# Loading a transpose's row blocks with every fourth row in the same quarter of the partitions, and mending the order with a permutation

## The chip, the cores and the metric

The kernel runs on one core of a Trainium2 chip. The metric is the device time in microseconds (us), the median of several runs. The core has engines with queues of their own, named as in the profile: TensorE (PE, with PEld for its weight loads), VectorE (DVE), ScalarE (ACT), GpSimd (POOL) and SyncE (SP). Transfers between the chip's memory and the core's on-chip memory run on 16 DMA engines, whichever queue issues them.

## The reference

The input is one matrix of 8192 x 8192 float32 (32 KB for a row, 268 MB in all). The output is its transpose.

```python
def reference(x: np.ndarray) -> np.ndarray:
    return np.transpose(x)
```

## The kernel before

The input is taken in 128 chunks `(s, c)`. Chunk `c` of strip `s` is a block of P = 128 rows (64 blocks, `CH`) by `J` = 4096 columns (two strips), so 2 MB, 16 KB in each of the 128 partitions. `load(t)` (L101) brings chunk `t` into one of `NIN` = 3 buffers `ins`, row `p` of the block into partition `p`. The first three loads are issued by SyncE, all others by ScalarE (L103).

`transposes(k)` (L112) waits until the semaphore of buffer `k` stands at 18: 16 from the transfer, and one each from ScalarE and VectorE, which say that they have emptied what the chunk before left in PSUM. Then TensorE transposes 32 blocks of 128 x 128, each by a matmul with the identity `ident` (L117). The columns of a block are taken in steps of `B` = 4, so that one partition of the result holds four neighbouring columns of `x`, which are four neighbouring rows of the output. `ident` is made by GpSimd at the start, from a memset and one select (L85, L87). TensorE's part is a loop with a register, the other engines' queues are written out in full.

ScalarE (for the first half, `e` = 0) and VectorE (`e` = 1) copy the results from PSUM into one of `NREG` = 9 regions of `regs` (L241). A region gathers one group of 512 output rows over up to `W` = 8 chunks; the eight groups are staggered, so that in the middle of the run about one region is complete after each chunk. `store` (L154) then writes it out, 2 MB at a time for full regions, 16 KB for each partition, to four output rows in pieces of up to 4 KB. All stores are issued by ScalarE.

In ScalarE's queue a store of chunk `t` waits until TensorE has begun chunk `t+1` (in the middle of the run), and `load(t + 3)` follows right behind it (L264). The transfers that ScalarE issues are thus ordered store, load, store, load, one pair for a chunk. SyncE waits for the last stores at the end (L266).

Transfers are made in two ways. `dma_start` needs the same shape on both sides. `wide_dma` (L25) adds the transfer instruction itself and hands it both access patterns as they are, with a count of 1 put in where a side has two dimensions only (`physical`), so the sides may have different shapes. All stores but the first go that way.

Of the kernel before, what the change touches and what calls it, by code (L numbers as in the profile page):

```python
# [8 lines left out]
def physical(ap):  # L9


    t = ap.tensor
    dims = [list(d) for d in ap.ap]
    if len(dims) == 2:
        dims.insert(1, [dims[1][1], 1])
    return mybir.PhysicalAccessPattern(
        ap=dims,
        offset=ap.offset,
        dtype=ap.dtype,
        memref=t.name,  # L20
        memsetref=t.name + "_set",
    )


def wide_dma(nc, eng, queue, out, in_):  # L25


    return eng.add_instruction(
        mybir.InstDMACopy(
            mode="Copy",  # L30
            name=nc.get_next_instruction_name(),
            engine=eng.engine,
            ins=[physical(in_)],
            outs=[physical(out)],
            queue=queue,
        )
    )
# [3 lines left out]
def kernel(  # L41
# [13 lines left out]
    nc = tc.nc  # L55
    P = 128
# [8 lines left out]
    NIN = 3  # L65
    NREG = 9
    CH = N // P
    J = S * P

    with tc.tile_critical():  # L70
        nc.alloc_sbuf_tensor("pad", [P, 32], dt)
        ident = nc.alloc_sbuf_tensor("ident", [P, P], dt).ap()
        ins = [nc.alloc_sbuf_tensor(f"in{k}", [P, J], dt).ap() for k in range(NIN)]
        SIZE = B * W * P
# [4 lines left out]
        s_id = nc.alloc_semaphore("s_id")  # L79
        s_ld = [nc.alloc_semaphore(f"s_ld{k}") for k in range(NIN)]  # L80
# [3 lines left out]

        nc.gpsimd.memset(ident, 0.0).then_inc(s_id, 1)  # L85
        nc.gpsimd.wait_ge(s_id, 1)
        nc.gpsimd.affine_select(  # L87
            out=ident,
            in_=ident,
            compare_op=mybir.AluOpType.not_equal,  # L90
            fill=1.0,
            base=0,
            pattern=[[-1, P]],
            channel_multiplier=1,
        ).then_inc(s_id, 1)
        nc.vector.sem_inc(s_ld[0], 1)
        nc.scalar.sem_inc(s_ld[0], 1)

        chunks = [(s, c) for s in range(M // J) for c in range(CH)]

        def load(t):  # L101
            s, c = chunks[t]
            (nc.sync if t < NIN else nc.scalar).dma_start(  # L103
                out=ins[t % NIN], in_=x[c * P:(c + 1) * P, s * J:(s + 1) * J]
            ).then_inc(s_ld[t % NIN], 16)

# [16 lines left out]
        T = len(chunks)  # L125
        assert T % NIN == NIN - 1
        pe = [nc.tensor.engine]
        nc.tensor.wait_ge(s_id, 2)

        turn = nc.alloc_registers("turn", engines=pe)  # L130
        nc.regs_mov(turn, 0)
# [11 lines left out]
        for t in range(NIN):  # L143
            load(t)
# [9 lines left out]
        def store(q, e, t):  # L154
# [7 lines left out]
            for s, a, z in parts:  # L162
                rows = (z - a) * P
                j0 = s * J + q * B * P
                dst = out[j0:j0 + B * P, a * P:a * P + rows]
# [19 lines left out]
        for t, (s, c) in enumerate(chunks):  # L185
            closed = []
            for e in range(2):
                eng = (nc.scalar, nc.vector)[e]
# [4 lines left out]
                for q in range(e * NH, (e + 1) * NH):  # L193
# [14 lines left out]
                    base = r * SIZE + B * P * sum(z - a for _, a, z in parts[:k])  # L208
# [52 lines left out]
            if t + NIN < T:  # L261
                if not closed:
                    nc.scalar.wait_ge(s_pe, (t + 1) * NH)
                load(t + NIN)  # L264
# [32 lines left out]
```

## Time and profile before

| | |
|---|---|
| median of 3 runs | 1261.94 us (1261.61 to 1261.95) |
| profiled execution, first to last instruction (span) | 1260.4 us |
| profiled execution, around the span, as median less span | 1.5 us |
| read from and written to memory | 268.44 MB and 268.44 MB |
| transfers issued | 270 |

The profile is of one execution. Its times are in us from the span's start unless they are marked ns; a row of a group of instructions gives their busy time, the mean of one, and the idle time of the engine ahead of them with what ended it. Rows of stretches give each engine's busy time with the number of instructions in brackets, the clock that TensorE was granted (1.00 is full speed), the busy share of the DMA engines and their rate. Rows of transfers give their number, the KB of one, and the median time from issue to landing. Registers, branches, semaphores and the issuing of transfers are not counted as busy.

### The profile page before, as it was taken

To read this page: it belongs to the slowest core of one execution; us is meant where nothing else is said; L and a number is where in the kernel's file an instruction comes from. 1 tells how busy PE (TensorE), PEld (TensorE's weight loads), DVE (VectorE), ACT (ScalarE), POOL (GpSimd) and SP (SyncE) were. 2 spreads that over 40 slices of the span, in tenths; PEclk is the share of its full clock that TensorE was granted. 3 is DMA by queue.
4 is the path that set the end of the run, shared out by engine and by line. 5 is a ranking of instruction groups with operands and counts; after the bars stand their busy time and mean duration, and the time that the engine had idled before them with its cause. 6 is when DMAs were issued, how large, how long until landed. Compare 5 with 4: busy or idle time off the path is not lost. (4 is left out here: it accounts for less than half of the span.)

```text
span 1260.4 us, 9367 instructions
## 1 busy us (share of the span) xinstructions
PE 739.0 (59%) x4096; PEld 718.4 (57%) x4096; DVE 302.0 (24%) x250; ACT 253.5 (20%) x257; POOL 0.7 (0%) x6
## 2 busy tenths in 40 slices
PE   5656556565566655565556656566565655665561
PEld 5556556565556655565555656565565655665561
DVE  2322222222222222222222222222222222222220
ACT  3212211122111211122111211121111211121110
POOL 0000000000000000000000000000000000000000
PEclk9886876868777777778687786867777687777776
DMA  9999999999999999999999999999999999999998
GB/s 383 429 422 426 425 430 431 426 431 431 427 430 431 428 428 431 428 429 432 427 422 426 429 429 425 431 429 428 430 428 428 431 428 429 429 429 429 429 431 376
DMA packets 39271, 536.95 MB, mean 426 GB/s; under 512 B 4320, under 2 KB 4832, under 8 KB 6240
## 3 DMA queue, kind: packets, MB, share of 16 engines
q10 hardware_dynamic: 38832, 530.60, 99.0%
q1 hardware_dynamic: 432, 6.29, 1.2%
q14 instruction: 6, 0.05, 0.0%
q8 instruction: 1, 0.02, 0.0%
HBM read 268.44 MB, written 268.44 MB: 426 GB/s over the span
## 5 line engine op out<-in xcount | busy, mean ns | idle before, releaser
L117 PE MATMUL ps<-ident,in 128*128 128x128 f32 x4096 | 739.0, 362 | 493.5 <-PEq L113 493.5
L117 PEld LDWEIGHTS ps<-ident,in 128*128 128x128 f32 x4096 | 718.4, 220 | 513.9 <-issue 513.9
L241 DVE COPY regs<-ps 128x512 f32<-128x512 f32 (+3 forms) x250 | 302.0, 1246 | 932.1 <-PE ps L117 932.1
L241 ACT COPY regs<-ps 128x512 f32<-128x512 f32 (+3 forms) x256 | 252.2, 1016 | 978.8 <-PE ps L117 760.8
L241 ACT ACT_TABLE_LOAD x1 | 1.3, 1283 | 1.0 <-SPq L70 1.0
L87 POOL TENSOR_SCALAR_AFFINE_SELECT ident<-ident 128x128 f32<-128x128 f32 x1 | 0.3, 293 | 0.2 <-POOL ident L85 0.2
L85 POOL MEMSET ident<- 128x128 f32 x1 | 0.2, 204 | 0.5 <-SPq L70 0.5
L281 POOL MEMSET const-bfloat16-1.0<- 128x1 bf16 x1 | 0.1, 102 | 0.0
L281 POOL MEMSET const-uint8-127<- 128x1 uint8 x1 | 0.1, 102 | 0.0
L281 POOL MEMSET const-float32-0.0<- 128x1 f32 x1 | 0.1, 99 | 0.2 <-issue 0.2
L281 POOL MEMSET const-float32-1.0<- 128x1 f32 x1 | 0.1, 99 | 0.0
## 6 DMA issues: line engine op xcount, KB each, us to landing
in<-in_x_dram ACTq DMA_DIRECT2D x125, 2048.0 KB, 16.8
out_dram<-regs ACTq DMA_DIRECT2D x114, 2048.0 KB, 12.6
out_dram<-regs ACTq DMA_DIRECT2D x4, 1792.0 KB, 11.1
in<-in_x_dram SPq DMA_DIRECT2D x3, 2048.0 KB, 11.7
out_dram<-regs ACTq DMA_DIRECT2D x4, 1536.0 KB, 12.5
out_dram<-regs ACTq DMA_DIRECT2D x4, 1280.0 KB, 11.5
out_dram<-regs ACTq DMA_DIRECT2D x4, 1024.0 KB, 11.1
out_dram<-regs ACTq DMA_DIRECT2D x4, 768.0 KB, 12.3
```

The costliest lines, as they stand in the source:

```text
L85: nc.gpsimd.memset(ident, 0.0).then_inc(s_id, 1)
L87: nc.gpsimd.affine_select(out=ident, in_=ident, compare_op=mybir.AluOpType.not_equal, fill=1.0, base=0, pattern=[[-1, P]], channel_multipl ...
L117: tr = nc.tensor.transpose(pss[e][:, (g * B + b) * P:(g * B + b + 1) * P], ins[k][:, q * B * P + b:(q + 1) * B * P - B + b + 1:B], ident,)
L241: cp = nc.scalar.copy(out=o, in_=i) if e == 0 else nc.vector.tensor_copy(out=o, in_=i)
L281: nc = _bacc.Bacc("TRN2", target_bir_lowering=False, num_devices=1)
```

## The change

In the loads, row `4 l + h` of a block now goes to partition `32 h + l`, for `h` from 0 to 3 and `l` from 0 to 31: each quarter of the partitions holds every fourth row. The source of a load is therefore a pattern of three dimensions, `(l h) j -> h l j`, with counts 4, 32 and 4096, and the loads after the first are made with `wide_dma`. Load 0 is split into four transfers of 32 partitions by 4096 elements; the first of them counts on the buffer's semaphore, the other three on a new one, `s_l0`, on which VectorE waits before its first signal to TensorE.

TensorE undoes the new order as it transposes: `ident` is no longer the identity but the permutation with a one in row `32 h + l` and column `4 l + h`, made with four selects of 32 partitions instead of one of 128. The transposes, copies and stores stay as they are.

```diff
+    H = 4
+    L = P // H
...
-        nc.gpsimd.affine_select(
-            out=ident,
-            in_=ident,
-            compare_op=mybir.AluOpType.not_equal,
-            fill=1.0,
-            base=0,
-            pattern=[[-1, P]],
-            channel_multiplier=1,
-        ).then_inc(s_id, 1)
+        for h in range(H):
+            nc.gpsimd.affine_select(
+                out=ident[h * L:(h + 1) * L, :],
+                in_=ident[h * L:(h + 1) * L, :],
+                compare_op=mybir.AluOpType.not_equal,
+                fill=1.0,
+                base=h,
+                pattern=[[-1, P]],
+                channel_multiplier=H,
+            ).then_inc(s_id, 1)
+        s_l0 = nc.alloc_semaphore("s_l0")
+        nc.vector.wait_ge(s_l0, 16 * (H - 1))
         nc.vector.sem_inc(s_ld[0], 1)
         nc.scalar.sem_inc(s_ld[0], 1)
...
         def load(t):
             s, c = chunks[t]
-            (nc.sync if t < NIN else nc.scalar).dma_start(
-                out=ins[t % NIN], in_=x[c * P:(c + 1) * P, s * J:(s + 1) * J]
-            ).then_inc(s_ld[t % NIN], 16)
+            src = x[c * P:(c + 1) * P, s * J:(s + 1) * J].rearrange("(l h) j -> h l j", h=H)
+            if t == 0:
+                for h in range(H):
+                    nc.sync.dma_start(out=ins[t][h * L:(h + 1) * L], in_=src[h]).then_inc(s_ld[0] if h == 0 else s_l0, 16)
+            else:
+                eng, queue = (nc.sync, "qSPDynamicHW") if t < NIN else (nc.scalar, "qActDynamicHW")
+                wide_dma(nc, eng, queue, ins[t % NIN], src).then_inc(s_ld[t % NIN], 16)
...
-        nc.tensor.wait_ge(s_id, 2)
+        nc.tensor.wait_ge(s_id, 1 + H)
```

## The prediction

> **What bounds the kernel now.** I read the page's busy shares and slices first, then the packets and queues, then stretches of the span, then the waits, and last the instructions in order of time.
>
> ```profile
> span 1260.4 us, 9367 instructions
> PE 739.0 (59%) x4096; PEld 718.4 (57%) x4096; DVE 302.0 (24%) x250; ACT 253.5 (20%) x257; POOL 0.7 (0%) x6
> DMA  9999999999999999999999999999999999999998
> GB/s 383 429 422 426 425 430 431 426 431 431 427 430 431 428 428 431 428 429 432 427 422 426 429 429 425 431 429 428 430 428 428 431 428 429 429 429 429 429 431 376
> DMA packets 39271, 536.95 MB, mean 426 GB/s; under 512 B 4320, under 2 KB 4832, under 8 KB 6240
> q10 hardware_dynamic: 38832, 530.60, 99.0%
> q1 hardware_dynamic: 432, 6.29, 1.2%
> HBM read 268.44 MB, written 268.44 MB: 426 GB/s over the span
> ```
>
> No computing engine is busy for more than 59% of the span, while the two transfer queues together keep the 16 DMA engines busy for 100%. The bytes are the least possible: 268.44 MB in and 268.44 MB out. So the time is bytes over rate, and the rate is flat:
>
> ```profile
> core 0: us, PE busy (x) PEld busy (x) DVE busy (x) ACT busy (x) POOL busy (x), PEclk, DMA share, GB/s
> 0.00:31.50 31.50, 17.80 (x128) 17.16 (x128) 8.57 (x14) 9.81 (x16) 0.70 (x6) 1.00 0.94 383
> 31.50:330.00 298.50, 178.50 (x1003) 173.52 (x1004) 73.57 (x52) 61.21 (x59) 0.00 (x0) 0.77 1.01 428
> ...
> 990.00:1229.00 239.00, 143.27 (x777) 139.43 (x778) 58.36 (x49) 46.89 (x45) 0.00 (x0) 0.75 1.01 429
> 1229.00:1260.40 31.40, 3.49 (x24) 3.30 (x23) 2.48 (x4) 2.34 (x4) 0.00 (x0) 0.61 0.90 377
> ```
>
> Only the first and the last 31 us are below a full share. Between them the share is 1.01 and the rate 428 to 429 GB/s, 26.8 GB/s for one engine. One engine moves 536.9/16 = 33.55 MB; at 428.2/16 = 26.76 GB/s that is 1253.7 us, and the other 6.7 us of the span are its two ends. The median of the runs, 1261.94 us, is 1.5 us over this span; I add that at the end.
>
> The waits agree: TensorE waits before each of the 128 chunks (the sequencer's wait on the loads), and SyncE does nothing but wait for stores.
>
> ```profile
> PE ps L117 <- PEq L113: 493.5, 128, 8.4
> SPq L266 <- DMA out_dram<-regs: 1256.8, 4, 1248.1
> ```
>
> **The change, part by part.** *How loads are cut into pieces.* Every transfer must be shared out over the 16 DMA engines. What before shows of that is a count:
>
> ```profile
> in<-in_x_dram ACTq DMA_DIRECT2D x125, 2048.0 KB, 16.8
> out_dram<-regs ACTq DMA_DIRECT2D x114, 2048.0 KB, 12.6
> out_dram<-regs ACTq DMA_DIRECT2D x4, 1792.0 KB, 11.1
> in<-in_x_dram SPq DMA_DIRECT2D x3, 2048.0 KB, 11.7
> ...
> out_dram<-regs ACTq DMA_DIRECT2D x4, 256.0 KB, 12.1
> ```
>
> There are 125 + 3 loads and 114 + 7 x 4 = 142 stores (seven smaller sizes, 1792 to 256 KB), 270 transfers, and 4320 packets under 512 B: exactly 16 for each transfer. I read these as one completion mark for each engine that took part, so each transfer of before ran in 16 pieces. In the code all 270 have a leading count of 128 or 512 on both sides, a multiple of 16. The simplest rule that fits is that a transfer is cut along the leading counts of its two sides, into a number of pieces, at most 16, that divides both.
>
> The change breaks the condition. Loads 1 to 127 now have the source `(l h) j -> h l j`: its leading count is H = 4, then 32 rows, then 4096 elements; the destination still leads with 128 partitions. Cut along leading counts, these loads make 4 pieces, one for each `h`: 32 rows of 16 KB on one engine. Sixteen pieces of eight partitions, which would start 32 rows x 32 KB = 1 MB apart, need the 4 and the 32 to be taken together. Load 0 is four transfers with a leading count of 32 on both sides, so it stays on 16 engines. The stores are untouched.
>
> [...]
>
> [...] A transfer in 16 pieces uses every engine, so before can't show which ones a smaller number takes; I take the same ones each time, as the simpler case, and keep the other as a rival. With k pieces on the same k engines, one of these engines carries 268.44/16 = 16.78 MB of stores and, for each of loads 1 to 127, 2.097/k MB, and 0.13 MB of load 0.
>
> For k = 4: 127 x 2.097/4 = 66.58 MB; with 16.78 and 0.13 it is 83.49 MB, 2.5 times as much as before. At 26.76 GB/s: 3119.9 us. With the ends, 6.7 us: a span of 3126.6 us. With 1.5 us around it: **3128 us**. For k = 16 it is before's 33.55 MB and 1260.4 us of span. In between there is no gentle case: k = 8 gives (16.78 + 33.43)/26.76 = 1876 us.
>
> Bounds on k = 4: the fastest slice, 432 GB/s or 27.0 GB/s for an engine, gives 3092 + 8 = 3100 us; no row shows one engine working with others idle, so I allow another 1% below. Above, the four engines must never run dry. What feeds them is ACT's queue:
>
> ```profile
> 610.74 6.12 PEld L117 LDWEIGHTS ps<-ident,in 128*128 128x128 f32 x32 [3.86 <-issue]
> 610.77 6.28 PE L117 MATMUL ps<-ident,in 128*128 128x128 f32 x32 [3.69 <-PEq L113]
> 612.75 0.55 ACTq L28 DMA_DIRECT2D out_dram<-regs  x1
> 613.34 0.61 ACTq L103 DMA_DIRECT2D in<-in_x_dram  x1
> 613.98 2.05 ACT L241 COPY regs<-ps 128x512 f32<-128x512 f32 x4 [7.72 <-issue]
> 617.08 2.48 DVE L241 COPY regs<-ps 128x512 f32<-128x512 f32 x4 [7.49 <-PE ps L117]
> ```
>
> When chunk t+1 has landed (610.7), the store of t and load t+3 are issued within 613.95 - 610.74 = 3.2 us. At that moment the store of t-1 and load t+2 are still queued: on a loaded engine 2.097/16/26.76 = 4.9 us and 2.097/4/26.76 = 19.6 us. A chunk is then 24.5 us, and TensorE (6.3), the copies and the issue (3.2) fit in it side by side. So these engines have over 20 us of work in hand, and I take no bubble. If they ran dry for the 3.2 us in every chunk, it would cost 127 x 3.2 = 406 us and end at 3530 us. What could do it is an issue that blocks: in the last stretch five store issues take 15.33 us in all, since the queues are full there.
>
> ```profile
> 1233.38 15.33 ACTq L28 DMA_DIRECT2D out_dram<-regs  x5
> ```
>
> [...]
>
> *The permutation, its wait and the split load 0.* These lie at the start:
>
> ```profile
> 0.94 1.32 SPq L103 DMA_DIRECT2D in<-in_x_dram  x3
> 1.38 0.29 POOL L87 TENSOR_SCALAR_AFFINE_SELECT ident<-ident 128x128 f32<-128x128 f32 x1 [0.23 <-POOL ident L85]
> 8.37 5.34 PEld L117 LDWEIGHTS ps<-ident,in 128*128 128x128 f32 x32 [8.37 <-issue]
> 13.94 0.36 ACTq L103 DMA_DIRECT2D in<-in_x_dram  x1
> ```
>
> Four selects in place of one are at most 4 x 0.29 us, 0.9 us more on POOL, done before 3 us; TensorE starts at 8.37 on load 0, so the price is nothing, and 0.9 us without that cover. SyncE issues six transfers instead of three, 3 x 0.44 = 1.3 us more, which puts loads 1 and 2 off, not the first piece. DVE's wait on `s_l0` has only DVE's sem_inc and its first copies behind it, and TensorE needs load 0 whole anyway. If load 0 lands 1 to 5 us later (its four pieces in turn, each a quarter of the partitions), the engines that decide still have loads 1 and 2 to carry, 39 us for k = 4: nothing. For k = 16 only two loads x 4.9 us are behind it and up to 2 us could show. The 4096 transposes keep their number, shape and order, and a permutation in place of the identity has the same operands.
>
> **The rivals.** *A: sixteen pieces after all, not slower.* The place is each load's split: if the inner 32 is taken with the 4, every engine gets eight rows, 33.55 MB as before, and the order in memory alone changes. It decides only at k = 16; at k = 8 the time is already 1876 us. For it speaks that 128 rows are there to be shared. Its gain is what ripple there is: the 38 inner slices average 428.4 GB/s, the usual best is 431, so 0.6% of 1197 us, 7 us, if loads caused all of it: 1255 us. If they caused none, 1262 us, with the first load's 0 to 2 us on top up to 1264. Against any large gain speaks that the engines are already full.
>
> *B: sixteen pieces, but reads 128 KB apart within an engine collide in memory.* All stores already write over that pitch at full rate, which speaks against it. If all slices fell to the slowest inner one, 422 instead of 428.2, it is 1.5%: 1281 us.
>
> *C: four pieces that go to other engines from load to load.* Then the stress spreads; with two loads in flight on eight engines the loaded ones would need about k = 8's 1876 us. Nothing in before rules it out; nothing shows it.
>
> **How the numbers follow.** A gets 0.10, B 0.02, C 0.03, and the four fixed engines 0.85: the counts in the code put a 4 where every transfer that was seen in 16 pieces had a multiple of 16, and cutting the leading count is the one rule that needs no regrouping. The time is that of four engines, 3128 us. The range is 3070 (the fastest slice's rate less 1%) to 3300 (under half of the dry-engine bound); I give it 0.95 if the four engines hold, so 0.81 in all. A measurement of this kernel can tell about 0.2%, 2.5 us, from no change. Slower: 0.85 + 0.02 + 0.03, and 0.01 from A; A leaves 0.06 for faster and 0.03 for the same.
>
> **What would show it.** Right: a mean rate of 537/3.127 = 172 GB/s and a DMA share about 0.4 (four engines full, twelve with 16.9 of 83.5 MB); packets under 512 B down from 4320 to 142 x 16 for stores, 4 x 16 for load 0 and 127 x 4: 2844; chunks of 24.5 us; TensorE's waits before a chunk near 18 us; a load about 46 us from issue to landing (two loads and two stores deep, 49 us, less the 2.6 from landing to issue). Wrong: 4320 + 48 tiny packets and a share of 1 (A or B); chunks well above 24.5 us with the share under 0.4 (dry engines); between 1500 and 2200 us (C). If the tiny packets are 2844 but one engine's rate differs from 26.76 GB/s, the cut was right and the rate was mis-sized.

## The result and the profile after

The changed kernel takes 3134.26 us (3133.94 to 3136.26) where the kernel before took 1261.78 us beside it: 2.484 times as long (95% interval 2.481 to 2.487). The prediction said 3128 us, in 3070 to 3300.

The page of the changed kernel, by the same rows as before: span and busy shares, the 40 slices of the DMA engines and their rate, packets, queues (q10 is ScalarE's, q1 SyncE's).

```profile
span 3132.4 us, 9376 instructions
PE 763.7 (24%) x4096; PEld 743.0 (24%) x4096; DVE 302.2 (10%) x250; ACT 252.8 (8%) x257; POOL 1.6 (0%) x9
DMA  3333334433443334433344333433344333443335
GB/s 105 151 166 167 168 168 183 171 168 168 173 183 168 168 167 177 180 168 168 168 186 170 168 167 168 186 168 168 168 178 178 168 168 167 181 176 168 168 171 249
DMA packets 37795, 536.95 MB, mean 171 GB/s; under 512 B 2844, under 2 KB 3356, under 8 KB 4764
q10 hardware_dynamic: 37332, 530.59, 39.8%
q1 hardware_dynamic: 456, 6.29, 0.7%
HBM read 268.44 MB, written 268.44 MB: 171 GB/s over the span
```

The bytes are the same, but the 16 engines are busy for 40% of the span in the mean instead of 100%. The small packets tell why: 2844 instead of 4320, which is 16 for each of the 142 stores and the four parts of load 0, and 4 for each of the other 127 loads. In a stretch from the middle, in order of time (start, duration, engine, what; idle time before in brackets):

```profile
1515.20 6.06 PE L126 MATMUL ps<-ident,in 128*128 128x128 f32 x32 [18.06 <-PEq L122]
1517.18 0.57 ACTq L28 DMA_DIRECT2D out_dram<-regs  x1
1517.79 0.58 ACTq L28 DMA_DIRECT2D in<-in_x_dram  x1
...
1539.50 5.89 PE L126 MATMUL ps<-ident,in 128*128 128x128 f32 x32 [18.24 <-PEq L122]
...
1563.79 5.71 PE L126 MATMUL ps<-ident,in 128*128 128x128 f32 x32 [18.41 <-PEq L122]
```

A chunk takes 24.3 us instead of 9.8. TensorE works for 6 us and waits 18 us for the next load. ScalarE issues here as promptly as before (0.57 and 0.58 us), so no issue blocks: the loaded engines set the pace. At the start the four parts of load 0 delay TensorE, and the next chunk comes late:

```profile
13.28 6.09 PE L126 MATMUL ps<-ident,in 128*128 128x128 f32 x32 [13.28 <-PEq L122]
46.69 6.39 PE L126 MATMUL ps<-ident,in 128*128 128x128 f32 x32 [27.32 <-PEq L122]
```

### The profile page after: what moved, and what is told of

The parts are those of the page before. It is cut to its first block, busy times and chain, and to the rows that moved or that the text cites. A ratio compares the mean times of both kernels' runs of the same rounds, so it can differ in the third digit from the quotient of the medians.

```text
span 3132.4 us, 9376 instructions
## 1 busy us (share of the span) xinstructions
PE 763.7 (24%) x4096; PEld 743.0 (24%) x4096; DVE 302.2 (10%) x250; ACT 252.8 (8%) x257; POOL 1.6 (0%) x9
## 2 busy tenths in 40 slices
DMA packets 37795, 536.95 MB, mean 171 GB/s; under 512 B 2844, under 2 KB 3356, under 8 KB 4764
## 3 DMA queue, kind: packets, MB, share of 16 engines
q10 hardware_dynamic: 37332, 530.59, 39.8%
## 5 line engine op out<-in xcount | busy, mean ns | idle before, releaser
L126 PE MATMUL ps<-ident,in 128*128 128x128 f32 x4096 | 763.7, 371 | 2341.5 <-PEq L122 2341.5
L126 PEld LDWEIGHTS ps<-ident,in 128*128 128x128 f32 x4096 | 743.0, 220 | 2361.9 <-issue 2361.9
```

What stands on the lines that cost most here:

```text
L126: tr = nc.tensor.transpose(pss[e][:, (g * B + b) * P:(g * B + b + 1) * P], ins[k][:, q * B * P + b:(q + 1) * B * P - B + b + 1:B], ident,)
```

## The experiments

The theory is that the leading counts of a transfer's two sides set the number of engines, and that loads with a leading 4 use the same four each time. The rivals: something else in the change costs the time (the form of the transfer, the permutation, the start), or the distance between the rows that one engine reads does.

**All of the change but the leading 4.**

```diff
-                wide_dma(nc, eng, queue, ins[t % NIN], src)...
+                wide_dma(nc, eng, queue, ins[t % NIN], x[c * P:(c + 1) * P, s * J:(s + 1) * J])...
```

> All of the change is kept (permutation, s_l0, load 0 in four transfers, wide_dma for loads 1 to 127), only the source of loads 1 to 127 is taken in its own row order again, so its leading count is 128 and not 4. (The rows within a block of 128 then stand in the permuted order in the output; times are not touched by that.) Theory, the cut follows the leading counts: 16 pieces again, 1262 us within 4 us, tiny packets 142 x 16 + 4 x 16 + 127 x 16 = 4368, DMA share about 1. Rival, the cost lies in wide_dma's form, the permutation or the start: it stays near 3134 us.

It took 1265.78 us, 1.0035 (1.0021 to 1.0049) of before, with the 4368 small packets forecast:

```profile
DMA packets 39319, 536.95 MB, mean 425 GB/s; under 512 B 4368, under 2 KB 4880, under 8 KB 6288
0.00:31.50 31.50, 14.38 (x96) 13.90 (x96) 6.29 (x11) 7.73 (x13) 1.56 (x9) 1.00 0.95 328
31.50:1229.00 1197.50, 721.08 (x3968) 701.07 (x3968) 293.35 (x236) 243.55 (x240) 0.00 (x0) 0.75 1.01 429
```

The second and third row are stretches of its span (busy times, granted clock, DMA share, GB/s). The middle is that of before; the 3.9 us that remain are the start, 328 GB/s in the first 31.5 us against 383. So the form of the transfer and the permutation cost nothing that can be seen, the start with its split load 0 about 4 us, and the leading 4 all the rest.

**Only the leading 4, rows and identity as before.** All loads go by `wide_dma` here and in the experiments with another H below, so a small `dma_start` into the unused tile `pad` stands ahead of them on SyncE's queue; the permutation is made by selects over all partitions, or is the identity (H = 1).

```diff
...
+            src = x[c * P:(c + 1) * P, s * J:(s + 1) * J].rearrange("(k l) j -> k l j", k=4)
...
```

> Rows in the order of the kernel before, with the identity; only the source pattern is written with leading counts 4 and 32 (32 neighbouring rows for each of 4 pieces). Theory, the leading count alone decides: 16.78 + 67.11 = 83.89 MB on an engine, 3135 us and with the ends 3143, within 15. Rival, the order of the rows in memory has a share in the changed kernel's 3134 us: lower than that by over 1%.

The one run took 3139.86 us, with 2928 small packets: 142 x 16 + 128 x 4, and 128 + 16 of the small transfer. The reordering of the rows has no part in the loss.

**Two pieces and eight pieces.** The second kernel has H = 8 in the same place.

```diff
-    H = 4
+    H = 2
...
```

> H = 2 in place of 4: every second row in the same half of the partitions; all loads by wide_dma, behind a small transfer into an unused tile; the permutation from selects over all partitions. Theory, cut along the leading count on the same engines each time: 2 pieces, 16.78 + 128 x 2.097/2 = 151.0 MB on an engine, at 26.76 GB/s 5642 us and with the ends 5650 us; tiny packets 142 x 16 + 128 x 2 + 16 = 2544; chunks 44.1 us. Rival, what costs is the distance between the rows that an engine reads (64 KB here, 128 KB with H = 4, 32 KB before): under 3134 us. Rival, pieces on engines that change from load to load: well under 5650 us.

> H = 8. Theory, cut along the leading count: 8 pieces, 16.78 + 33.55 = 50.33 MB on an engine, 1881 us and with the ends 1889 us; tiny packets 142 x 16 + 128 x 8 + 16 = 3312. Rival, the distance between the rows that an engine reads (256 KB here): over 3134 us.

In one run each, H = 2 took 5607.58 us, 0.75% under its forecast, and H = 8 1922.55 us, 1.8% over; small packets 2672 and 3440, the forecasts plus the 128 of the small transfer. If distance between rows were what costs, H = 2 would have been the fastest of the three, and it is the slowest. The bytes of the busiest engine order all of them. That H = 2 needs the full 5.6 ms also means that its pieces do not move over to idle engines from load to load.

At the start the number of engines is seen directly. From 4 to 22 us only the first loads move, on SyncE's queue. The rows give packets, MB and the share of 16 engines, for H = 2, for the leading 4 with the rows of before, and for H = 8; the last line is H = 8's rate by slices:

```profile
q1 hardware_dynamic: 60, 0.98, 12.7%
q1 hardware_dynamic: 70, 1.15, 24.9%
q1 hardware_dynamic: 137, 2.11, 50.5%
GB/s 121 160 263 273 290 289 281 286 297 281 281 292 291 281 283 300 280 281 294 290 280 281 297 283 281 284 300 281 281 294 289 280 286 297 281 281 294 289 303 305
```

These are 2, 4 and 8 engines of 16, although with 4 and 8 pieces all three first loads had been issued by 3.5 us. One engine moved 0.98 MB in 0.127 x 16 x 18 us, 26.8 GB/s, with two pieces, but by the same sum only 16.0 with four and 14.5 with eight. The slices of H = 8 show this slow start, and that it passes; it is why H = 8 came out over its forecast. Why it passes no run here shows.

**Sixteen pieces.**

```diff
-    H = 4
+    H = 16
...
```

> H = 16: the leading count is 16, so by the theory 16 pieces of 8 rows that lie 512 KB apart, 33.55 MB on every engine: 1262 us, tiny packets 142 x 16 + 128 x 16 + 16 = 4336. Rival, distance between rows: slower than H = 8. Second rival: with this cut an engine has 8 neighbouring partitions, and if engines then meet at the same part of the on-chip memory as load 0's four transfers seem to in the changed kernel (first transposes at 13.2 instead of 8.4 us), loads run at down to half rate: between 1262 and 1889 us.

The four runs took 1745, 1752, 1822 and 1852 us, inside the range of the second rival (1262 to 1889), though the cut is in 16 (4464 small packets, 4336 + 128). The page of the run of 1745 us:

```profile
span 1743.3 us, 9400 instructions
DMA  9999999999999999999999999999999999999998
DMA packets 39415, 536.97 MB, mean 308 GB/s; under 512 B 4464, under 2 KB 4976, under 8 KB 6384
q10 hardware_dynamic: 38832, 530.60, 98.3%
```

All engines are busy all the time, as before, yet move 308 GB/s. By the queue's row, 16 KB take 0.983 x 16 x 1743.3 us x 16 KB / 530.60 MB = 0.85 us of an engine, against 0.62 by the same row of before. So packets are held up while they count as busy. Two things may be at work: rows of one engine are 512 KB apart instead of 32 (theory M, memory), or, if the cut follows the leading 16, each engine has eight neighbouring partitions and engines meet there (theory P, on-chip memory). The next two kernels separate them. The first has the rows of before (H = 1).

```diff
...
+            src = x[c * P:(c + 1) * P, s * J:(s + 1) * J].rearrange("(k l) j -> k l j", k=16)
...
```

> Rows in the order of the kernel before, with the identity; only the source pattern is written with leading counts 16 and 8 (eight neighbouring rows for each of 16 pieces) and all loads go by wide_dma, behind a small transfer into an unused tile. It asks why H = 16 took 1745 to 1852 us with full engines and packets of 16 KB at a mean of 0.86 us instead of 0.61. Theory P, engines meet in on-chip memory, because a cut in 16 along a leading 16 gives each engine eight neighbouring partitions: the same here, 1740 to 1860 us. Theory M, it is memory, rows of one engine 512 KB apart with H = 16: here they are 32 KB apart as before, so 1262 us.

```diff
-    H = 4
+    H = 32
...
```

> H = 32: leading counts 32 and 4; every 32nd row, 1 MB apart, goes to the same four neighbouring partitions. Packets 142 x 16 + 128 x 16 + 16 under 512 B plus some 128 for the small transfer, so 16 pieces. [...] Theory P with a plain cut of 32 in 16 (eight neighbours again): 1740 to 1860 us. Theory M: rows 1 MB apart, no faster than H = 16, over 1740 us.

With rows next to each other but a leading 16, so by theory P eight neighbouring partitions for each engine: 1770.02 us. With rows 1 MB apart and a leading 32, for which 1262 us within 5 was forecast if the engines do not meet: 1271.44 us. Pages of the first and the second:

```profile
DMA packets 39415, 536.97 MB, mean 305 GB/s; under 512 B 4464, under 2 KB 4976, under 8 KB 6384
```

```profile
GB/s 312 411 426 429 426 430 430 429 428 428 429 431 429 431 429 430 428 429 430 429 424 427 429 431 429 430 428 430 430 430 427 430 430 430 430 430 428 430 428 365
DMA packets 39416, 536.98 MB, mean 424 GB/s; under 512 B 4464, under 2 KB 4976, under 8 KB 6384
```

Theory M fails on both. Theory P fits both only if with a leading 32 or 128 the engines get their partitions otherwise than with 16. That was the author's assumption: no trace shows which partitions an engine serves, or where engines meet. Measured are the times, 1745 to 1852 us with a leading 16 against 1262 with 128 and 1271 with 32.

The start shows the loads by themselves. From 4 to 13 us nothing moves but the first loads: in the kernel before, with the leading 16 and the rows of before, with H = 32, and in the first experiment, where load 0 is in four parts:

```profile
q1 hardware_dynamic: 267, 3.85, 99.9%
q1 hardware_dynamic: 136, 2.00, 103.2%
q1 hardware_dynamic: 256, 3.93, 102.0%
q1 hardware_dynamic: 185, 1.98, 99.1%
```

All engines are full in all four, and in the second and the fourth they move half the bytes. No store takes part, so the pieces of the loads hold each other up; it is not the neighbours in one engine as such, since with H = 2 each engine had 64 of them by the same cut and ran at 26.8 GB/s. The four parts of load 0 are of this kind, and that is where the 4 us of the first experiment went.

**The change's order of rows, on 16 engines, by four transfers for each load.**

```diff
+            for h in range(H):
+                (nc.sync if t < NIN else nc.scalar).dma_start(
+                    out=ins[t % NIN][h * L:(h + 1) * L], in_=src[h]
+                ).then_inc(s_ld[t % NIN], 16)
...
+            nc.tensor.sem_inc(s_ld[k], -16 * H - 2).wait_op(s_ld[k], 16 * H + 2, "sem-ge")
```

> The changed kernel's order of rows and its permutation, but each load made as load 0 is: four transfers of 32 partitions, each with a leading count of 32 on both sides, so 16 pieces; a buffer's semaphore counts to 66. Tiny packets 142 x 16 + 512 x 16 = 10464. If the number of pieces were all: 1262 to 1275 us. [...]

By theory P, with loads at down to half rate, 1700 to 1890 us were forecast, since load 0 made this way landed 4.9 us late. Two runs took 1714.49 and 1810.51 us. The engines are full and slow again; the page is of the longer run:

```profile
span 1808.7 us, 9757 instructions
q10 hardware_dynamic: 44832, 530.62, 98.7%
DMA packets 45418, 537.00 MB, mean 297 GB/s; under 512 B 10464, under 2 KB 10976, under 8 KB 12384
```

So the split that spares load 0 the leading 4 is the slow kind as well. A transfer over 32 partitions reaches a quarter of them, and theory P would have its 16 engines meet there; measured are 297 GB/s at a share of 98.7% for ScalarE's queue.

**Rows far apart without the late start.** H = 32 made its permutation with 32 selects, and TensorE waited for them:

```profile
13.66 1.61 POOL L90 TENSOR_SCALAR_AFFINE_SELECT ident<-ident 128x128 f32<-128x128 f32 x4 [0.17 <-POOL ident L90]
15.88 5.75 PE L121 MATMUL ps<-ident,in 128*128 128x128 f32 x32 [15.88 <-PEq L117]
```

One select over a view of the columns does the same; it also serves H = 64.

```diff
+        nc.gpsimd.affine_select(
+            out=ident.rearrange("p (l h) -> p l h", h=H),
+            in_=ident.rearrange("p (l h) -> p l h", h=H),
...
+            pattern=[[-1, L], [-L, H]],
+            channel_multiplier=1,
+        ).then_inc(s_id, 1)
```

> H = 32 with the permutation made by one select over a view of its columns instead of 32 selects. With 32 of them TensorE began at 15.9 us instead of 8.4 and the first two slices had 312 and 411 GB/s; between the ends the rate was 427 to 430 GB/s, as before. If the late start was what made H = 32 slower (1271 us, before 1262): TensorE starts at 8.4 to 9 us and the time is 1259 to 1264 us, the same as before within 0.2%. If rows 1 MB apart cost something of their own: still over 1267 us. If they help: under 1259 us.

> H = 64, leading counts 64 and 2, rows 2 MB apart in two neighbouring partitions, one select as well. [...]

TensorE began at 9.2 us. H = 32: 1262.96 us, 1.0008 (0.9995 to 1.0021) of before. H = 64, forecast at 1259 to 1264 us as well: 1262.27 us, 1.0003 (0.9987 to 1.0018). H = 32 by stretches:

```profile
0.00:31.50 31.50, 17.24 (x121) 16.79 (x122) 7.45 (x12) 9.16 (x15) 0.72 (x6) 1.00 0.91 369
31.50:1229.00 1197.50, 724.32 (x3953) 704.30 (x3953) 292.06 (x234) 241.98 (x239) 0.00 (x0) 0.74 1.01 429
```

429 GB/s in the middle, against 428 in the same stretch of before: reading 1 or 2 MB apart neither helps nor hurts by more than some 0.2%. No version tried here beats the kernel before.

## Why the prediction was right

*The bound.* That the DMA engines set the time held: TensorE waits 18 us in each chunk as forecast. That nothing would be added held but for the start, below.

*The cut.* The step on which all hung, 4 pieces for a leading 4, is shown three ways: 2844 small packets as counted ahead; the time back to 1266 us when the leading count alone is restored; 3140 us when it alone is changed. The small packets of the runs fit a cut along the leading count: 2, 4 and 8 for each load with a leading 2, 4 and 8 (2672, 2844 and 3440 in all), and 16 with 16, 32 and 128 (4464, 4464 and 4320). That each piece is an engine the busy shares at the start agree with, 12.7%, 24.9% and 50.5% of 16; so a transfer is not always shared out over all 16.

*The same engines each time.* Taken as the simpler case, without a row for it. The sum for fixed engines came out within 2% for H = 2, 4 and 8, and with three loads issued no more than 4 or 8 engines worked, so rival C is out. Which ones they are no run here shows.

*The rate.* 83.49 MB on the busiest engine in 3132.4 - 6.7 us is 26.71 GB/s, against the 26.76 taken from before. In the middle a full engine works as in before: by the queue's row of the page, 16 KB take 0.398 x 16 x 3132.4 us x 16 KB / 530.59 MB = 0.62 us. A chunk takes 24.3 us there and not 24.5: (3099.18 - 46.69)/126 = 24.23 us in the mean by the starts of chunk 1 and of the last chunk, below. Over 126 chunks that is 33 us less, but little of it is won: another 33 us pass after the last start, in which 10.14 MB of stores are still moved (last line).

The start is the term that the sum lacks, some 13 us. Chunk 1, due when load 0 (13.3) and its own 19.6 us are over, at 33 us, began at 46.7. Load 3, which ScalarE issues at 19.4 us, is not the cause: from there to 46.7 us its queue, q10, moved 0.05 MB. SyncE's queue, q1, kept four engines full, 24.6% of 16, and moved 1.82 MB, 16.9 GB/s for one engine: the slow start seen above with four and eight pieces. It fits theory P, but by theory P alone the loss should go on in the middle, where there is none; this stays open. That the span is only 5.8 us over the forecast is in part luck: without the late start it would have come out some 8 us under. The rows of queues are those from 19.4 to 46.7 us and from 3099.2 us to the end:

```profile
19.40 1.13 ACTq L28 DMA_DIRECT2D in<-in_x_dram  x1
q1 hardware_dynamic: 115, 1.82, 24.6%
q10 hardware_dynamic: 107, 0.05, 1.1%
...
3099.18 5.97 PE L126 MATMUL ps<-ident,in 128*128 128x128 f32 x32 [18.15 <-PEq L122]
q10 hardware_dynamic: 1202, 10.14, 73.2%
```

*Dry engines.* No bubble was taken, and none is there; the 406 us of that bound were not needed. The issue that blocks stays at the end, where it was: five store issues take 14.89 us from 3105.71 on, against 15.33 before. How full a queue is no row shows; the engines were full while those issues of before ran, with a share of 1.00 from 1233 to 1249 us. A load's time from issue to landing, forecast at 46 us, is in no row of the page, but the stretch from the middle gives it: the load issued at 1517.79 is the one for which TensorE waits until 1563.79, 46.0 us later. A store's time went from 12.6 to 27.0 us:

```profile
out_dram<-regs ACTq DMA_DIRECT2D x114, 2048.0 KB, 27.0
```

*The start.* The selects cost 1.1 us under load 0, nothing, as said. That load 0 could land 1 to 5 us later was right, 4.9 us (13.28 against 8.40). Its price, "up to 2 us" for 16 pieces, was too low: 3.9 us in the first experiment. And for four pieces it was not the split alone that made the start late, as said above.

*Rivals A and B* did not come about, and what distance alone does is measured too. A's gain of up to 7 us from the order in memory isn't there, nor is B's loss: 1.0008 and 1.0003 of before with sixteen pieces and rows 1 and 2 MB apart. At the 128 KB of the change no run separates them from the partitions. The statement that the time is decided by k alone, with 16 pieces as good as before, was wrong: H = 16 and the four transfers have 16 pieces and take 1.4 times as long. The prediction's formula has no term for that; by theory P it would be which partitions an engine gets.

## What to carry to other kernels

Before reordering a transfer's rows by its access pattern, look at the leading count on both sides: it, and not the number of rows, set how many DMA engines worked here, and the count of small packets for each load showed it in the profiles: 2, 4, 8 or 16. Keep all 128 partitions in one transfer, with a leading count that kept the full rate here (32, 64 or 128 beside 128 partitions: 429, 429 and 428 GB/s in the middle); 16 (1745 to 1852 us), or four transfers of 32 partitions (1714 and 1811 us), kept all engines busy and still took about 1.4 times as long. A queue's share of 98 to 99% went with 308 and 297 GB/s in these and with 426 in before, so a full share is no proof of full rate: read the GB/s beside it.

## What the runs showed that was not expected

Full engines moved 305 GB/s instead of 428 with nothing changed in the rows, only a leading 16 in place of 128 (1770 us), and half the bytes of before while loads ran alone. With four and eight pieces the loads start just as slowly (16.0 and 14.5 GB/s for one engine, against 13.5 with sixteen) and then reach the full rate (with eight, 287 GB/s at a share of 0.67, 26.8 for one engine); with sixteen pieces by a leading 16 they stay slow. What makes the difference is open. And an engine did not run faster here when others idled for most of the time: with 2 engines loaded, 150.99 MB in 5605.8 - 6.7 us is 26.97 GB/s, as with 16 at their best (432/16 = 27.0).
